# A roll along the columns: row pieces moved from two hardware DMA queues to the software ring

## The chip, the cores and the metric

The kernel runs on one core of one Trainium2 chip. The core has compute engines (TensorE, VectorE = DVE, ScalarE = ACT, GpSimd = POOL, and SyncE = SP, which only issues and waits) and 16 DMA engines that move data between the chip's main memory (HBM) and the core's working memory (SBUF), or from HBM to HBM. A DMA is issued by an instruction of SP, ACT or POOL, goes into that engine's queue, and is carried out by the DMA engines. The metric is the device time of one execution in microseconds. Before the change the median of three runs is 828.71 us (828.44 to 829.27).

## The reference

`x` is a float32 matrix of 8192 x 8192, `shift` is 100:

```python
def reference(x, shift):
    return np.roll(x, shift, axis=1)
```

So each output row is the input row turned by 100 places: `out[r, 100:] = x[r, :8092]` and `out[r, :100] = x[r, 8092:]`. There is no arithmetic; 268.44 MB are read and 268.44 MB are written.

## The kernel before

With `s = 100`, `a` is the next multiple of 128 above it, 128, and `g = a - s = 28`. Each output row is made of two parts.

*The long piece*: `out[r, 128:]` is `x[r, 28:8092]`, 8064 elements or 32,256 bytes. It goes from HBM to HBM directly (line L41). The rows are cut into 128 blocks `c` of 64 rows, and a block's row is named by `e` (0 to 15) and `j` (0 to 3): row `64c + 4e + j`. For each block there is one DMA for each `j`, over all 16 `e`, so that each of the 16 DMA engines gets one row of it. SP issues those with even `j`, ACT those with odd `j`. In the last four blocks each row is cut at column `mid = 4096`, and each half has a DMA of its own. SP and ACT issue 264 DMAs each: 248 of 504 KB, and 16 of 248 or 256 KB. On each of the two queues four DMAs are in flight: the next waits until the one four before it has landed.

*The head*: `out[r, :128]`, 512 bytes, is the end of row `r` (100 elements) followed by its beginning (28 elements). These go through SBUF, in 16 stages `k` of 512 rows, each partition `p` holding four successive rows `q`. Since the end of one row and the start of the next lie side by side in memory, one load (L70, tile `t`) reads 128 elements across each of the three row borders inside a partition's four rows. The end of the fourth row (L71) and the start of the first (L74) are loaded by themselves into the tile `h`. DVE copies the parts of `t` to their places in `h` (L72: ends, L75: starts). After all 16 stages of loads, 16 stores (L78) write the heads, `h` to `out[:, :128]`. All of these DMAs are issued by POOL, on the software ring, and are marked `single_packet=True`.

The order on POOL is the order of the program. Its ring has eight semaphores, taken in turn, so each POOL DMA waits until the one eight before it has landed; a store also waits for DVE's copies. Tiles have a buffer for each stage, so nothing waits for a buffer. SP's and ACT's queues and the POOL ring are independent of each other, since heads and long pieces write different bytes.

The queues have these names in the profile: q1 and q10 are the two hardware queues (SP's and ACT's; q10 is the one that began first, with ACT), q0 is the software ring of POOL, and q14 loads the program.

Of the kernel before, what the change touches and what calls it, by code (L numbers as in the profile page):

```python
# [1 line left out]

# [4 lines left out]


@with_exitstack
def kernel(  # L10
    ctx: ExitStack,
    tc: tile.TileContext,
    x: bass.AP,
    shift: int,
    out: bass.AP,
):
    nc = tc.nc
    n_rows, n_cols = x.shape
    s = shift % n_cols
    a = -(-s // 128) * 128  # L20
    g = a - s
    P = nc.NUM_PARTITIONS
    engines = [nc.sync, nc.scalar]
    n_chunks = 16
    rows = n_rows // n_chunks

    xm = x.rearrange("(c e j) w -> c j e w", e=16, j=4)
    om = out.rearrange("(c e j) w -> c j e w", e=16, j=4)
    if a < n_cols:
        blocks = n_rows // 64
        mid = (a + n_cols) // 256 * 128
        for c in range(blocks):
            parts = ((a, mid), (mid, n_cols)) if c >= blocks - 4 and a < mid else ((a, n_cols),)
            for j in range(4):
                for lo, hi in parts:  # L40
                    engines[j % 2].dma_start(out=om[c, j, :, lo:hi], in_=xm[c, j, :, lo - s:hi - s])  # L41
    if a == 0:
        return


    if a > 512:
        for i in range(n_chunks):
            r = slice(i * rows, (i + 1) * rows)
            nc.gpsimd.dma_start(out=out[r, :s], in_=x[r, n_cols - s:])
            if g > 0:  # L50
                nc.gpsimd.dma_start(out=out[r, s:a], in_=x[r, :g])
        return

    Q = 4
    n_st = n_rows // (P * Q)
    reads = ctx.enter_context(tc.tile_pool(name="reads", bufs=n_st))  # L60
    heads = ctx.enter_context(tc.tile_pool(name="heads", bufs=n_st))
    xt = x.rearrange("(k p q) c -> k p q c", q=Q, p=P)
    ot = out.rearrange("(k p q) c -> k p q c", q=Q, p=P)
    tiles = []
    for k in range(n_st):
        t = reads.tile([P, Q - 1, a], x.dtype)
        h = heads.tile([P, Q, a], x.dtype)
        lead = bass.AP(tensor=x.tensor, offset=(k * P * Q + 1) * n_cols - s,
                       ap=[[Q * n_cols, P], [n_cols, Q - 1], [1, a]])
        nc.gpsimd.dma_start(out=t[:], in_=lead, single_packet=True)  # L70
        nc.gpsimd.dma_start(out=h[:, Q - 1, :s], in_=xt[k, :, Q - 1, n_cols - s:], single_packet=True)  # L71
        nc.vector.tensor_copy(h[:, :Q - 1, :s], t[:, :, :s])  # L72
        if g > 0:
            nc.gpsimd.dma_start(out=h[:, 0, s:], in_=xt[k, :, 0, :g], single_packet=True)  # L74
            nc.vector.tensor_copy(h[:, 1:, s:], t[:, :, s:])  # L75
        tiles.append(h)
    for k, h in enumerate(tiles):
        nc.gpsimd.dma_start(out=ot[k, :, :, :a], in_=h[:], single_packet=True)  # L78


# [1 line left out]
_INS = ['x', 'shift']  # L82
_OUTS = [((8192, 8192), 'float32')]

_NUMBERS = {'shift': 100}


# [26 lines left out]
```

## Time and profile before

| | before |
|---|---|
| median of the runs | 828.71 us (828.44 to 829.27) |
| span of the profiled execution (first to last instruction) | 818.3 us |
| around the span, against the median | 10.4 us |
| POOL busy | 41.1 us |
| DVE busy | 7.8 us |
| data moved by the DMA engines | 272.71 MB, mean 333 GB/s |
| HBM traffic, read and written | 536.9 MB, 656 GB/s over the span |
| one POOL issue: L70, L71, L74, L78 | 759, 558, 538, 712 ns |
| issue to landing: rows of 504 KB, heads `t`, stores of `h` | 12.5, 32.6, 63.0 us (medians) |

The profiled execution's own device time is not listed beside the others; its span is 818.3 us, and it is compared with the median of the runs. In the list of the queues, the share is the time that a queue's packets took, as a part of 16 engines' time; a row of windows has the stretch and its length, the busy time of DVE and POOL with their instructions, the granted clock, the DMA engines' busy share and the rate in GB/s. A row that goes from HBM to HBM counts once in the DMA rate and twice in the HBM traffic (read and write). A row of waits has who waited for what, the total in us, how often, and the longest.

### The profile page before, as it was taken

Reading aid. Unit: us, or ns where it says so; the run is one execution under the profiler, and the core shown is the slowest. Engines: PE = TensorE matmul, PEld = TensorE weight load, DVE = VectorE, ACT = ScalarE, POOL = GpSimd, SP = SyncE. Lnnn points to the kernel's source line nnn. Section 1 sums busy time; section 2 is a strip of 40 time slices with the busy share of each in tenths; the row PEclk is TensorE's granted clock in tenths of the full one; section 3 lists DMA queues with packets and bytes.
Section 4 is the critical chain, followed back from the end, with each engine's and each line's share of the span. In section 5 each row is a group of like instructions: output and inputs, shape, how many; then the busy total and the mean of one; then the engine's idle time right before and its main releaser. Section 6 shows DMA issues by size and latency. Waiting matters only on the chain. (4 is left out here: it accounts for less than half of the span.)

```text
span 818.3 us, 689 instructions
## 1 busy us (share of the span) xinstructions
DVE 7.8 (1%) x32; POOL 41.1 (5%) x68
## 2 busy tenths in 40 slices
DVE  0000000000000000000000000000000000000000
POOL 3011111111010000000000000000000000000000
DMA  9999999999999999999999999999999999999998
GB/s 304 340 344 338 341 334 345 341 346 350 353 352 357 347 332 321 335 328 326 333 330 323 330 331 330 331 326 333 330 328 334 333 330 339 328 333 334 328 318 294
DMA packets 20229, 272.71 MB, mean 333 GB/s; under 512 B 9472, under 2 KB 9728, under 8 KB 11776
## 3 DMA queue, kind: packets, MB, share of 16 engines
q1 hardware_dynamic: 8448, 132.14, 48.2%
q10 hardware_dynamic: 8448, 132.14, 46.1%
q0 software_dynamic: 3328, 8.39, 4.7%
q14 instruction: 5, 0.04, 0.0%
HBM read 268.44 MB, written 268.44 MB: 656 GB/s over the span
## 5 line engine op out<-in xcount | busy, mean ns | idle before, releaser
L78 POOL DMA_DIRECT2D out_dram<-h x16 | 11.4, 712 | 87.2 <-DMA out_dram<-h 51.7
L70 POOL DMA_DIRECT2D t<-in_x_dram x16 | 12.1, 759 | 32.1 <-DMA h<-in_x_dram 31.3
L74 POOL DMA_DIRECT2D h<-in_x_dram x16 | 8.6, 538 | 85.7 <-DMA t<-in_x_dram 85.7
L71 POOL DMA_DIRECT2D h<-in_x_dram x16 | 8.9, 558 | 23.9 <-DMA h<-in_x_dram 23.9
L72 DVE COPY h<-t 128x300 f32<-128x300 f32 x16 | 5.9, 368 | 190.4 <-DMA t<-in_x_dram 190.4
L75 DVE COPY h<-t 128x84 f32<-128x84 f32 x16 | 3.2, 201 | 0.0
L95 POOL MEMSET const-float32-0.0<- 128x1 f32 x1 | 0.1, 99 | 0.2 <-issue 0.2
L95 POOL MEMSET const-bfloat16-1.0<- 128x1 bf16 x1 | 0.1, 101 | 0.0
L95 POOL MEMSET const-uint8-127<- 128x1 uint8 x1 | 0.1, 99 | 0.0
L95 POOL MEMSET const-float32-1.0<- 128x1 f32 x1 | 0.1, 98 | 0.0
## 6 DMA issues: line engine op xcount, KB each, us to landing
out_dram<-in_x_dram ACTq DMA_DIRECT2D x248, 504.0 KB, 12.5
out_dram<-in_x_dram SPq DMA_DIRECT2D x248, 504.0 KB, 12.5
out_dram<-h POOLq DMA_DIRECT2D x16, 256.0 KB, 63.0
t<-in_x_dram POOLq DMA_DIRECT2D x16, 192.0 KB, 32.6
out_dram<-in_x_dram SPq DMA_DIRECT2D x8, 256.0 KB, 5.9
out_dram<-in_x_dram ACTq DMA_DIRECT2D x8, 256.0 KB, 5.8
out_dram<-in_x_dram SPq DMA_DIRECT2D x8, 248.0 KB, 6.1
out_dram<-in_x_dram ACTq DMA_DIRECT2D x8, 248.0 KB, 6.1
```

The source lines that it names most:

```text
L70: nc.gpsimd.dma_start(out=t[:], in_=lead, single_packet=True)
L71: nc.gpsimd.dma_start(out=h[:, Q - 1, :s], in_=xt[k, :, Q - 1, n_cols - s:], single_packet=True)
L72: nc.vector.tensor_copy(h[:, :Q - 1, :s], t[:, :, :s])
L74: nc.gpsimd.dma_start(out=h[:, 0, s:], in_=xt[k, :, 0, :g], single_packet=True)
L75: nc.vector.tensor_copy(h[:, 1:, s:], t[:, :, s:])
L78: nc.gpsimd.dma_start(out=ot[k, :, :, :a], in_=h[:], single_packet=True)
L95: nc = _bacc.Bacc("TRN2", target_bir_lowering=False, num_devices=1)
```

## The change

All DMAs are now issued by POOL on the software ring; SP and ACT issue none. The long pieces of a block of 64 rows are one DMA, `[16, 4, 8064]`, marked as a single packet: each DMA engine gets four successive rows. There are 128 of these, of 2,016 KB each. The last blocks are no longer cut in halves. The heads keep their stages, loads, copies and stores, but they are woven between the long pieces: in each stage `k` of 512 rows come one long-piece DMA, the three loads of the heads, seven long-piece DMAs, and the store of the heads of stage `k - 2` (`lag = 2`). After the last stage the two stores that are left follow. POOL issues 192 DMAs in all, each of which waits for the one eight before it.

```diff
-    engines = [nc.sync, nc.scalar]
...
-    xm = x.rearrange("(c e j) w -> c j e w", e=16, j=4)
-    om = out.rearrange("(c e j) w -> c j e w", e=16, j=4)
-    if a < n_cols:
-        blocks = n_rows // 64
-        mid = (a + n_cols) // 256 * 128
-        for c in range(blocks):
-            parts = ((a, mid), (mid, n_cols)) if c >= blocks - 4 and a < mid else ((a, n_cols),)
-            for j in range(4):
-                for lo, hi in parts:
-                    engines[j % 2].dma_start(out=om[c, j, :, lo:hi], in_=xm[c, j, :, lo - s:hi - s])
+    J = 4
+    xm = x.rearrange("(c e j) w -> c e j w", e=16, j=J)
+    om = out.rearrange("(c e j) w -> c e j w", e=16, j=J)
+    blocks = n_rows // (16 * J)
+
+    def long_pieces(c):
+        if a < n_cols:
+            nc.gpsimd.dma_start(out=om[c, :, :, a:], in_=xm[c, :, :, a - s:n_cols - s], single_packet=True)
...
     Q = 4
     n_st = n_rows // (P * Q)
+    per = blocks // n_st
+    lag = 2
...
-    tiles = []
-    for k in range(n_st):
+    def read_heads(k):
         t = reads.tile([P, Q - 1, a], x.dtype)
         h = heads.tile([P, Q, a], x.dtype)
...
-        tiles.append(h)
-    for k, h in enumerate(tiles):
-        nc.gpsimd.dma_start(out=ot[k, :, :, :a], in_=h[:], single_packet=True)
+        return h
+
+    tiles = []
+    for k in range(n_st):
+        long_pieces(k * per)
+        tiles.append(read_heads(k))
+        for i in range(1, per):
+            long_pieces(k * per + i)
+        if k >= lag:
+            nc.gpsimd.dma_start(out=ot[k - lag, :, :, :a], in_=tiles[k - lag][:], single_packet=True)
+        if k == n_st - 1:
+            for m in range(n_st - lag, n_st):
+                nc.gpsimd.dma_start(out=ot[m, :, :, :a], in_=tiles[m][:], single_packet=True)
```

The loads and copies inside `read_heads` are those of before, unchanged.

More of the change, by code (lines that the diff above doesn't have):

```diff
@@ L22 @@
     P = nc.NUM_PARTITIONS
-    engines = [nc.sync, nc.scalar]
-    n_chunks = 16
-    rows = n_rows // n_chunks
-    xm = x.rearrange("(c e j) w -> c j e w", e=16, j=4)
-    om = out.rearrange("(c e j) w -> c j e w", e=16, j=4)
-    if a < n_cols:
-        blocks = n_rows // 64
-        mid = (a + n_cols) // 256 * 128
-        for c in range(blocks):
-            parts = ((a, mid), (mid, n_cols)) if c >= blocks - 4 and a < mid else ((a, n_cols),)
-            for j in range(4):
-                for lo, hi in parts:
[L41 to L49, printed above, removed]
+    J = 4
[5 more added lines that the diff above has]
+            nc.gpsimd.dma_start(out=om[c, :, :, a:], in_=xm[c, :, :, a - s:n_cols - s], single_packet=True)
+    if a == 0 or a > 512:
+        for c in range(blocks):
+            long_pieces(c)
+            r = slice(c * 16 * J, (c + 1) * 16 * J)
+            if s > 0:
+                nc.gpsimd.dma_start(out=out[r, :s], in_=x[r, n_cols - s:])
             if g > 0:
```

## The prediction

> **What bounds the kernel now.** I read the page first: the share of the engines and of the 16 DMA engines, then the queues.
>
> ```profile
> span 818.3 us, 689 instructions
> DVE 7.8 (1%) x32; POOL 41.1 (5%) x68
> DMA  9999999999999999999999999999999999999998
> q1 hardware_dynamic: 8448, 132.14, 48.2%
> q10 hardware_dynamic: 8448, 132.14, 46.1%
> q0 software_dynamic: 3328, 8.39, 4.7%
> HBM read 268.44 MB, written 268.44 MB: 656 GB/s over the span
> ```
>
> No compute engine matters; the DMA engines are busy from end to end (48.2 + 46.1 + 4.7 = 99%). That is not yet a bound: a packet's time contains what it waits for. So, second, the windows and the queues by window (columns of a queue: packets, MB, share of 16 engines).
>
> ```profile
> 2.00:20.00 18.00, 0.48 (x2) 6.06 (x11) 1.00 1.00 331
> 20.00:170.00 150.00, 5.83 (x24) 22.19 (x37) 1.00 0.99 340
> 200.00:265.00 65.00, 0.00 (x0) 6.39 (x9) 1.00 1.00 353
> 300.00:780.00 480.00, 0.00 (x0) 0.00 (x0) 1.00 1.00 330
> 780.00:800.00 20.00, 0.00 (x0) 0.00 (x0) 1.00 0.90 315
> 800.00:817.00 17.00, 0.00 (x0) 0.00 (x0) 1.00 0.94 314
> ```
>
> Of 20 to 170 us (heads are loaded beside the rows), then 200 to 265 (heads are stored), 300 to 780 (rows alone), 802 to 816 (half rows alone), and 2 to 4 (the first rows):
>
> ```profile
> q1 hardware_dynamic: 1476, 23.94, 44.0%
> q10 hardware_dynamic: 1456, 23.36, 39.9%
> q0 software_dynamic: 1804, 3.73, 15.4%
> ...
> q1 hardware_dynamic: 634, 10.19, 46.2%
> q10 hardware_dynamic: 638, 10.36, 43.5%
> q0 software_dynamic: 715, 2.34, 10.4%
> ...
> q1 hardware_dynamic: 4912, 79.23, 50.5%
> q10 hardware_dynamic: 4912, 79.23, 49.2%
> ...
> q1 hardware_dynamic: 282, 2.18, 49.5%
> q10 hardware_dynamic: 281, 2.31, 49.0%
> ...
> q10 hardware_dynamic: 20, 0.52, 83.1%
> ```
>
> A row piece is read from HBM and written to HBM, a head crosses HBM once in each of its two steps. So HBM moved 2 x 47.30 + 3.73 = 98.3 MB in 150 us, 656 GB/s; then 2 x 20.55 + 2.34 = 43.4 MB in 65 us, 668 GB/s; then 2 x 158.46 + 0.07 = 317 MB in 480 us, 660 GB/s. The DMA figure changes by stage (340, 353, 330), the HBM traffic does not. And an engine is not at its own limit: a row of the ACT queue (q10) took 39.9% x 16 x 150 us / 23.36 MB x 32,256 B = 1.32 us while heads were loaded, 49.2% x 16 x 480 / 79.23 x 32,256 B = 1.54 us without. So I take the bound to be the memory, at 656 to 668 GB/s, with some 12% of room on each engine (1.32 against the mean of 1.50).
>
> Third, who waits for whom.
>
> ```profile
> SPq L41 <- DMA out_dram<-in_x_dram: 671.1, 260, 4.8
> POOL out_dram L78 <- DMA out_dram<-h: 51.7, 7, 9.1
> ```
>
> SP waits for an earlier DMA of its own nearly all the time: the queues are full and issuing is free. Rows land 12.5 us after their issue (page, part 6), four DMAs deep on each queue, so no engine can be more than about 8 rows ahead of the slowest. POOL's ring is eight DMAs deep.
>
> **The change, part by part.** All sums start from the profiled execution's 818.3 us; the median of the runs is 828.71, so 10.4 us lie around the span (program load before the first instruction), and I leave that unchanged.
>
> 1. *Issue.* 512 row pieces leave as 128 DMAs of 64 rows instead of 528 on SP and ACT. SP's and ACT's issues cost nothing now (they wait 671 us), so taking them away gives 0. On POOL one such issue is bounded by its own rows: 0.54 us (L74) to 0.76 (L70); I take 0.6. 128 x 0.6 + 41 = 118 us in 818, while each 64-row DMA (2.06 MB) lasts 6.2 us at 330 GB/s. Hidden by the full ring: 0.
>
> 2. *Waits on POOL.* Each DMA now waits for the one eight before it, and everything queues behind that wait. In the new order any eight neighbours hold at least four row DMAs (store, three head loads, row DMAs for the rest), so at least 3 x 6.2 = 18 us of work is queued when a wait ends, against 0.6 us to issue. The store of head k-2 also waits for DVE (0.37 + 0.20 us of copies), whose loads were issued a stage of 8 x 6.2 = 50 us earlier. 0.
>
> 3. *Heads on the same ring, spread over the run.* The bytes are the same. At their own pace heads take 15.4% x 16 x 150 / 3.73 = 99 us of engine time per MB, 8.39 MB x 99 / 16 = 52 us an engine at most (the page's 4.7% gives 38), and rows at 1.32 us need 512 x 1.32 = 676; 728 together is under 818, so the engines still wait for memory. 0, as long as engines reach their heads at different times.
>
> 4. *Packets of four rows, a quarter of the completions.* Bounds from the half rows: there a row took 2 x 16,128 B at 2.18 MB / (49.5% x 16 x 14 us) = 19.7 and 2.31 / (49.0% x 224) = 21.0 GB/s, 1.59 us against 1.50 whole. If all of the 0.09 us is the price of one more packet and its completion, three of four saved give 512 x 3/4 x 0.09 = 35 us. At the other end it is nothing: that window is 14 us near the end, at 4.49 x 2 / 14 = 641 GB/s, and windows of that length swing as much (315 at 780 to 800, 331 at 2 to 20, where rows are whole). If the memory is the bound, saved engine time returns as waiting. I take 0 and keep 35.
>
> 5. *One ring instead of three.* No row in this trace follows another row of its own ring, so overlap within a ring is not shown. Below, a gain could only be the packet price of step 4, already kept there. Above, each row could cost what the first ones did, with nothing fetched ahead: 83.1% x 32 us = 26.6 us for 16 rows, 1.66 us. Then 512 x 1.66 + 38 + 6 = 894. I take 0, since the first rows also hold the cold start, and keep the end.
>
> 6. *Start.* The first row packet is at 2.14 us, 1.40 us after ACT's issue at 0.74. POOL's first issue is at 1.28 us and its first packet at 5.07, behind one row of each other queue. So the start moves by 1.28 + 1.40 - 2.14 = 0.5 to 5.07 - 2.14 = 2.9 us; I take 1.5. The Trainium skill (DMA: Bandwidth & Descriptors, Latency and other measured facts) puts the first byte at about 1 us on the software path and 0.6 on the hardware path; by it the start would move by 0.54 + 0.4 = 0.9 us and the sum would be 0.6 lower.
>
> 7. *End.* Now the last four blocks go in halves, which shrinks the window and draws the engines together: 315 instead of 330 GB/s for 20 us and 314 for 17 cost (15 x 20 + 16 x 17) / 330 = 1.7 us. Afterwards nothing does. The last instruction waits for the DMA eight before it, with five row DMAs (20 rows an engine) and three stores behind: an engine may finish as much as 20 x 1.32 + 3 x 0.76 = 28.7 us after the first (a store: 10.4% x 1040 us / 2.34 MB x 16 KB = 0.76). Bounds 0 and 28.7. The landings of one row DMA spread now over 6 to 8 us of the 12.5, half the window; half of 28.7 is 14 us of lag, evenly spread over the engines 7 us of work each. Together that is 7 x 16 x 24.4 GB/s / 330 = 8.3 us of memory time, but the last engine needs 14: a loss of 5.7. I take +5.7 - 1.7 = +4.0 (-1.7 to +27).
>
> Sum: 818.3 + 1.5 + 4.0 = 823.8 us of span, 834.2 of device time, +0.7%.
>
> **The rivals.** 0.2% (1.7 us) is about what can be told from no change.
>
> *Faster: the packet costs.* If a packet and its completion hold the engine for up to 0.09 us and the engine, not the memory, sets the pace, step 4 pays in full: 834.2 - 35 = 799. For it: 99% busy, half rows slower. Against it: 656 to 668 GB/s in every stage. It decides from 5.5 us on, that is 0.014 us a row.
>
> *Slower: engines drift to the edge of the window.* If one or two engines are steadily slower, the deep ring lets the others run off, and the end costs the full 27: 857. For it: POOL's eight-deep ring shows waits of 9.1 us between stores. Against it: the 12% of room that lets a late engine catch up. The Trainium skill has such a rule (same page and section): engines 7 and 15 are usually slower, its best guess being traffic to the software path's descriptor rings. No view here separates the engines.
>
> *Much slower: a ring does not overlap its rows.* Step 5: 894 of span, 904. Against it: the rate would have to fall below what the whole trace shows for queued rows.
>
> *No change.* If the engines stay within a few us, start and end cancel (+1.5 - 1.7): about 829. That the grouping does nothing is part of this and of the forecast: the packet records of q0, issued as single packets already, are of 4 KB, with rows of other queues between.
>
> **How the numbers follow.** Forecast 0.38, its own range 830.4 to 842; faster 0.27 (799 to 827); no change 0.10 (827 to 830.4); drift 0.12 (842 to 858); no overlap 0.13 (858 to 904). So faster 0.27, same 0.10, slower 0.38 + 0.12 + 0.13 = 0.63. The range leaves out no overlap (0.13) and the lower quarter of faster (0.07): 806 to 858.
>
> **What would show it.** Step 1: POOL about 118 us busy, its waits on earlier DMAs long. Steps 3 to 5: HBM 656 to 668 GB/s in the middle windows, and a row near 1.5 us on q0; under 1.45 speaks for packet costs, 1.6 or more for a ring that does not overlap. Step 6: the first window short by some 1.5 us of work. Step 7: the last 20 us fall off in steps of idle engines. The forecast is wrong if the middle rate moves by over 1%, which is 8 us.

## The result and the profile after

The change makes the kernel slower: 871.57 us median (852.17 to 879.3, four runs) against 828.66 us for the kernel before in runs beside it. The changed kernel's runs lie far apart, and the ratio is taken over those within 1.5% of the quickest, here two of the four: 1.035, with a 95% interval of 1.028 to 1.043, or some 29 us. By the medians it is 1.052.

One correction belongs ahead of the comparison. The profiled execution of the changed kernel took 864.1 us with a span of 862.3, so only 1.8 us lie around a span. The 10.4 us that the prediction set around the span of the kernel before were mostly another thing: with 1.8 us around its span of 818.3, its profile is from an execution of about 820 us. Beside the experiments the kernel before ran in 818.2 us on one chip and in 828.9 and 830.3 us on another, 1.3% apart. So the two profiles are compared by shares and shapes, and times on the chip of the changed kernel's runs: there a span of the kernel before is some 828.66 - 1.8 = 826.9 us, and the changed kernel's is 35.4 us longer.

The page of the changed kernel:

```profile
span 862.3 us, 285 instructions
DVE 7.8 (1%) x32; POOL 106.8 (12%) x196
DMA  9999999999999989999999999999989999899991
q0 software_dynamic: 13568, 272.64, 95.0%
HBM read 268.44 MB, written 268.44 MB: 623 GB/s over the span
```

POOL is still far from being the bound. But the DMA engines are no longer busy throughout: 95% instead of 99%, with two places where it is lost. The windows show both (length, busy time of DVE and POOL, clock, share of the DMA engines, GB/s):

```profile
2.00:20.00 18.00, 0.48 (x2) 6.26 (x12) 1.00 1.00 335
20.00:170.00 150.00, 0.97 (x4) 15.98 (x30) 1.00 1.00 329
170.00:300.00 130.00, 1.45 (x6) 16.86 (x30) 1.00 0.98 330
...
300.00:780.00 480.00, 4.37 (x18) 60.00 (x108) 1.00 0.96 320
780.00:836.00 56.00, 0.48 (x2) 6.82 (x12) 1.00 0.98 325
836.00:842.00 6.00, 0.00 (x0) 0.00 (x0) 1.00 0.87 318
842.00:858.00 16.00, 0.00 (x0) 0.00 (x0) 1.00 0.11 43
858.00:862.00 4.00, 0.00 (x0) 0.00 (x0) 1.00 0.00 0
```

Up to 170 us the engines are full. From then on 2 to 4% of their time is empty, although POOL waits most of the time (the two longest rows alone make 475 us) for an earlier DMA to land, that is, with its ring full:

```profile
POOL out_dram L31 <- DMA out_dram<-in_x_dram: 388.4, 76, 6.9
POOL t L57 <- DMA out_dram<-in_x_dram: 86.6, 15, 6.7
```

And from 842 to 858 us a rate of 43 GB/s at a share of 0.11 is one or two engines of sixteen at work. What happens is seen in the times at which the sixteen engines report one DMA done; the trace doesn't say which engine a report is from. These are the landings of single row DMAs, each in us after its first one, sorted:

```
kernel before, DMA of one row an engine, first landing at 592 us
  0.0 0.4 0.6 0.9 1.0 1.0 1.5 2.5 4.5 5.2 5.4 5.5 5.5 5.5 5.6  6.9
changed kernel, DMA of four rows an engine, first landing at 116 us
  0.0 0.5 0.6 0.7 1.3 1.5 1.7 1.8 1.9 3.4 3.5 3.7 4.6 4.8 9.5 12.6
at 209 us
  0.0 1.3 2.1 2.3 2.5 2.7 3.5 4.2 4.3 4.5 4.6 4.9 5.1 6.7 17.1 20.1
at 601 us
  0.0 0.0 0.1 0.3 0.4 0.4 0.6 0.7 1.1 1.1 1.5 1.6 1.7 2.3 5.8 22.0
at 815 us
  0.0 0.0 0.2 0.6 0.9 0.9 1.1 1.3 1.3 1.4 1.6 2.0 2.2 2.3 2.8 20.9
```

One engine, at first two, falls behind, within some 100 us, to about 20 us (16 to 25 over all DMAs from 170 us on), and stays there. I call it the straggler, and take the last landing of each DMA as its own: an engine 20 us behind can't make that up within a DMA of some 6 us, so it is the same engine from one DMA to the next. That distance is the depth of the ring: a DMA is issued only when the one eight before it has landed everywhere, and the prediction had counted at least 18 us of work in that window. So the other engines run into its edge, wait for the straggler, and at the end, from 842 us on, it has some 16 us of work left when the others have none. Its last rows, alone, take 1.194 us each.

The same trace shows what the straggler loses its time with. Steps between its landings, by kind of DMA, against those of the bunch (means over the 31st to the 185th DMA, when it is behind):

```
                       t load   100-element load   28-element load   head store   row DMA
straggler                2.93               1.61              0.20         1.48      5.89
median of the others     0.56               0.24              0.21         0.85      6.37
```

Heads cost it 6.2 us a stage, the others 1.9; at rows it is not slower, and the others' 6.37 us contain their waits for it. Eight row DMAs and the heads of a stage make 8 x 5.89 + 6.2 = 53.3 us for the straggler, and sixteen such stages 853 us: its own work fills the run.

The packet records say which short pieces are slow. I take those that start last before the straggler's landing as its own (means over twelve stages). In the `t` loads they are 4,096 bytes long and took 1.12 us, where the bunch's took 0.23; in the 100-element loads, 3,200 bytes, 1.58 us against 0.20. In the stores, again 4,096 bytes, they took 0.26 us against 0.18. So it is the two longer loads that are slow beside the other engines' rows: a packet with an eighth of a row's bytes takes three quarters of a row's time (1.53 us), or all of it.

What this costs is read from the HBM traffic, since an engine's idle time costs nothing while the others keep the memory busy. The DMA queue from 20 to 170 and from 300 to 780 us:

```profile
q0 software_dynamic: 2323, 49.28, 99.9%
...
q0 software_dynamic: 7645, 153.68, 96.1%
```

By the packets' lengths 48.25 and 148.96 MB of these are rows, which cross HBM twice, and the rest heads. That makes (2 x 48.25 + 1.03) / 150 = 650 GB/s and then (2 x 148.96 + 4.73) / 480 = 630. The kernel before on this chip has 536.9 MB in 826.9 us, 649 GB/s. So nothing is lost up to 170 us, nor up to 300 (651 GB/s). Against 650 GB/s the loss is 14.4 us from 300 to 780, 0.8 to 836, and 15.2 in the lonely end from 836 to 858. The last landing is at 857.9, and from there to the end of the span it is 4.4 us instead of 1.0, of which more below; the start costs 0.5. Together that is 34.3 of the 35.4 us.

### The profile page after: what moved, and what is told of

Its sections match the earlier page's. It is cut to its first block, busy times and chain, and to the rows that moved or that the text cites. A ratio compares the mean times of both kernels' runs of the same rounds, so it can differ in the third digit from the quotient of the medians.

```text
span 862.3 us, 285 instructions
## 1 busy us (share of the span) xinstructions
DVE 7.8 (1%) x32; POOL 106.8 (12%) x196
## 2 busy tenths in 40 slices
DMA packets 13570, 272.66 MB, mean 316 GB/s; under 512 B 3072, under 2 KB 3328, under 8 KB 5376
## 3 DMA queue, kind: packets, MB, share of 16 engines
q0 software_dynamic: 13568, 272.64, 95.0%
## 4 chain that ended last, share of the span: by engine, by line
DMA 95%; issue 1%; POOL 0%; POOLq 0%; PEldq 0%
DMA out_dram<-in_x_dram 63%; DMA t<-in_x_dram 32%; POOL out_dram L31 0%; POOL t L57 0%; POOLq L106 0%; POOL h L58 0%; POOL h L61 0%; PEldq L106 0%; POOLq L75 0%
## 5 line engine op out<-in xcount | busy, mean ns | idle before, releaser
L31 POOL DMA_DIRECT2D out_dram<-in_x_dram x128 | 64.5, 505 | 456.8 <-DMA out_dram<-in_x_dram 388.4
L72 POOL DMA_DIRECT2D out_dram<-h x14 | 10.4, 743 | 1.0 <-issue 0.4
## 6 DMA issues: line engine op xcount, KB each, us to landing
h<-in_x_dram POOLq DMA_DIRECT2D x16, 50.0 KB, 34.3
```

The lines of the kernel that those rows point to most:

```text
L31: nc.gpsimd.dma_start(out=om[c, :, :, a:], in_=xm[c, :, :, a - s:n_cols - s], single_packet=True)
L72: nc.gpsimd.dma_start(out=ot[k - lag, :, :, :a], in_=tiles[k - lag][:], single_packet=True)
```

## The experiments

All are edits of the changed kernel, and ratios are to the kernel before on the same chip.

**Everything on SP's hardware ring.** The edit, in all DMAs:

```diff
-nc.gpsimd.dma_start(...)
+nc.sync.dma_start(...)
```

> The changed kernel with every DMA issued by SP on its hardware ring: same order, same sizes, same eight-deep window, nothing on POOL. In the changed kernel's trace one engine lands each row DMA some 20 us after the other fourteen or fifteen, from 180 us on to the end, the others wait for it (DMA share 0.96) and it finishes 22 us alone. Theory A (the software ring slows one engine): no straggler here, HBM 655 to 665 GB/s in the middle, no lonely end, 826 to 838 us. Theory B (any single ring eight deep drifts like this): the straggler is there, 850 to 875 us. Theory C (long pieces of four rows are slow by themselves): also 850 or more, but with all engines alike.

Measured: 879.63 us against 818.19, ratio 1.067 (1.062 to 1.072). That is above what I had given for theory B, too. The straggler is there, in the rows from 150 us on 12 to 17 us behind. Of its page, and of its window from 300 us:

```profile
DMA packets 29698, 272.66 MB, mean 309 GB/s; under 512 B 7168, under 2 KB 21504, under 8 KB 21504
q1 hardware_dynamic: 29696, 272.64, 93.2%
```

```profile
300.00:780.00 480.00, 3.88 (x16) 0.00 (x0) 1.00 0.94 309
```

Theory A falls: the software ring is not the cause, and on the hardware ring the loss is not smaller. The packets say one thing more: the same transfers made 13,568 packets on the software ring and 29,696 here. The software ring groups the heads' short pieces into packets of up to 4,096 bytes, the hardware ring moves them in packets of 512, 400 and 112 bytes, though they are marked `single_packet` on both.

**The last blocks cut in halves**, as they were before the change:

```diff
-            nc.gpsimd.dma_start(out=om[c, :, :, a:], in_=xm[c, :, :, a - s:n_cols - s], single_packet=True)
+            if c < blocks - 4:
+                nc.gpsimd.dma_start(out=om[c, :, :, a:], in_=xm[c, :, :, a - s:n_cols - s], single_packet=True)
+            else:
+                for j in range(J):
+                    for lo, hi in ((a, 4096), (4096, n_cols)):
+                        nc.gpsimd.dma_start(out=om[c, :, j, lo:hi], in_=xm[c, :, j, lo - s:hi - s], single_packet=True)
```

> The changed kernel with the last four blocks cut into half rows, as before the change, all on the software ring, so that the window shrinks to eight half rows at the end. If the loss at the end is one of the wide window (step 7 of the prediction: engines apart when the work runs out), the last engine ends within 5 to 8 us of the others and the time falls by 13 to 17 us against the changed kernel, to 840 to 848 in its quick runs. If one slow engine sets the pace, it has the same rows to do, and the others only wait earlier: the lonely end goes, a slower stretch before it comes, and the time falls by 0 to 5 us.

Measured: 854.42 against 818.19, ratio 1.044 (1.042 to 1.046). This is the second of the two cases: the landings of the last DMA lie within 0.8 us, and yet there is no gain to be seen against the 1.035 and (below) 1.042 of the uncut kernel, which was not run on this chip and whose runs lie far apart. The windows show where the loss went:

```profile
300.00:780.00 480.00, 4.36 (x18) 60.06 (x108) 1.00 0.96 325
780.00:800.00 20.00, 0.00 (x0) 2.55 (x5) 1.00 0.94 321
800.00:820.00 20.00, 0.49 (x2) 2.91 (x6) 1.00 0.57 189
820.00:840.00 20.00, 0.00 (x0) 12.31 (x26) 1.00 0.84 285
```

From 800 to 820 us the engines are 0.57 busy: the others wait for the straggler there instead of after 840. A tighter end does not give back what an engine is behind; it has to do its rows either way.

**Rows alone.** Loads, copies and stores of the heads are left out, so the first 128 columns of the output are not written:

```diff
-        tiles.append(read_heads(k))
...
-        if k >= lag:
-            nc.gpsimd.dma_start(out=ot[k - lag, :, :, :a], in_=tiles[k - lag][:], single_packet=True)
...
```

> The changed kernel without the heads: their loads, DVE copies and stores are left out, so the first 128 columns of the output are not written. 528.5 MB of HBM traffic remain, 803 us at 658 GB/s, with start and end some 818 to 822 of device time. If the software ring itself makes an engine slow, the straggler is still there: 620 to 635 GB/s in the middle and a lonely end, 835 to 865 us. If the heads (short pieces, SBUF) in the same ring make it, it is gone: 815 to 824 us.

Measured: 821.37 against 818.19, ratio 1.004 (1.001 to 1.007). No straggler: the engines stay within 2 to 9 us of each other to the end.

```profile
300.00:780.00 480.00, 36.91 (x74) 1.00 1.00 330
812.00:817.00 5.00, 0.00 (x0) 1.00 0.00 0
```

330 GB/s is what the kernel before does with rows alone. So four rows of an engine in one DMA on one ring are neither better nor worse than single rows on two, and it is the heads in line with them that make the straggler. The second line is the end: the last landing is at 811.8 us, the span ends at 817.8.

**Row by row.** One DMA for each `j`, still on the software ring:

```diff
-            nc.gpsimd.dma_start(out=om[c, :, :, a:], in_=xm[c, :, :, a - s:n_cols - s], single_packet=True)
+            for j in range(J):
+                nc.gpsimd.dma_start(out=om[c, :, j, a:], in_=xm[c, :, j, a - s:n_cols - s], single_packet=True)
```

> The changed kernel with one DMA per row of an engine (16 rows each, 512 DMAs) on the software ring: the grouping of four rows is undone, the window shrinks to eight rows. If grouping or the wide window costs the time, this comes back to 826 to 836 us. If one engine is slow on the software ring whatever the grouping, the middle stays at 620 to 635 GB/s and only the lonely end shrinks, to some 6 to 8 us: 838 to 865 us. POOL issues 512 x 0.5 us more, 260 us in all, which is hidden either way.

Measured: 830.47 against 818.19, ratio 1.0145 (1.012 to 1.017).

```profile
300.00:780.00 480.00, 4.66 (x20) 172.59 (x340) 1.00 1.00 335
820.00:830.00 10.00, 0.00 (x0) 0.00 (x0) 1.00 0.10 38
```

The heads are in line as in the change, but the window is a quarter as deep, and no engine is more than 3 to 8 us behind. The engines are full (1.00, 335 GB/s against 325 for the cut end above, on the same chip with the same work). Most of the loss of the change is gone, then. This edit makes the DMAs smaller along with the window; since rows alone lose nothing by DMAs of four rows, I put it down to the window, but four-row DMAs with fewer in flight were not tried. Of the 12 us that remain, 3.5 are the end (last landing 825.3, end of the span 829.8, against 1.0 before).

**The change once more**, beside the kernels that follow:

> The changed kernel once more, beside the runs that it is compared with. The chip of the first experiments runs the kernel before in 818 us instead of 829. If the loss is a share of the time, 1.03 to 1.06 of the kernel before here too, with the same straggler some 20 us behind the others.

Measured: 877.89 us (864.01 to 886.4) against 828.92; 1.042 for the quickest run, 1.059 for the median. The straggler is 19 to 27 us behind, and the engines' share from 300 us on is a little lower still:

```profile
300.00:780.00 480.00, 3.88 (x16) 57.73 (x104) 1.00 0.95 312
```

**Heads on SP.** The edit, in `read_heads` and the stores alone:

```diff
-nc.gpsimd.dma_start(...)
+nc.sync.dma_start(...)
```

> The changed kernel with the heads' loads and stores issued by SP on its hardware ring; the row pieces stay on the software ring, four rows to an engine, eight DMAs deep. Rows alone on that ring had no straggler. If it is the heads standing in line with the rows that make one, it stays away here, HBM is at 655 to 665 GB/s in the middle and the time is 1.00 to 1.015 of the kernel before. If the heads make one engine slow wherever they stand, there is a straggler again and 1.03 or more.

Measured: 866.43 against 828.92, ratio 1.042 (1.036 to 1.048). This answered another question than the one asked. The page's queue and its issues, and the queue from 832 us to the end:

```profile
q1 hardware_dynamic: 19456, 8.39, 4.0%
...
t<-in_x_dram SPq DMA_DIRECT2D x16, 192.0 KB, 105.2
```

```profile
q1 hardware_dynamic: 7949, 3.53, 37.1%
```

The heads take 19,456 packets on this ring instead of 3,328, and a load needs 105 us to land, where it needed 33 before the change. (That each short packet waits its turn behind a row's packet would account for it, but the trace doesn't name the engines and so doesn't show it.) The heads fall behind the rows, and 3.53 of their 8.39 MB are moved after 832 us, when the rows are nearly done. Nor are the rows together: their landings spread over 20 us at 206 and 44 at 721 us, this time over all engines rather than with one straggler. That is more than rows show with no heads beside them (9 us above, 18 us in the next experiment). So a ring of its own does not keep the engines together when the rows' window is deep.

**Heads apart.** All loads after the first row DMA, all stores at the end, same ring:

```diff
+    long_pieces(0)
     for k in range(n_st):
-        long_pieces(k * per)
         tiles.append(read_heads(k))
-        for i in range(1, per):
-            long_pieces(k * per + i)
...
+    for c in range(1, blocks):
+        long_pieces(c)
+    for k in range(n_st):
+        nc.gpsimd.dma_start(out=ot[k, :, :, :a], in_=tiles[k][:], single_packet=True)
```

> The changed kernel with all head loads right after the first row DMA and all head stores at the very end, in the same software ring: the rows in between have no heads among them. In the changed kernel the straggler's heads of a stage take 2.93 + 1.61 + 0.20 us for the loads and 1.48 for the store, the others' 0.56 + 0.24 + 0.21 and 0.85. If its heads are slow because the others are busy with rows meanwhile, here all engines do heads together and quickly: 16 x 1.0 us of loads, 16 x 0.85 of stores, no straggler over 8 us in the rows, 1.03 to 1.04 of the kernel before, most of the loss now being memory that idles in the two blocks of heads. If one engine is slow at heads by itself, the loads alone take 16 x 4.7 = 75 us and the stores 24, 1.09 or more.

Measured: 865.28 against 828.92, ratio 1.045 (1.042 to 1.048), a little above the range.

```profile
10.00:42.00 32.00, 8.41 (x32) 28.60 (x49) 1.00 0.63 186
300.00:780.00 480.00, 0.00 (x0) 37.38 (x75) 1.00 1.00 325
846.00:862.00 16.00, 0.00 (x0) 7.31 (x10) 1.00 0.80 260
```

In the 48 loads, 10 to 37 us, no engine is more than 0.9 us behind the first: no engine is slow at heads when nobody does rows. The first stages, which were queued already, land 0.9 us apart, the later ones at POOL's pace of issue (28.6 us busy of 32), which I had not reckoned with. In the rows there is no straggler either, but four engines run ahead of twelve, by 12 us at 616 us, and from first to last it is 18 us in the end: rows drift apart by themselves too, at no loss here (share 1.00). The time is lost as expected, with the memory half idle in the heads: 186 GB/s for 32 us, and those are bytes that cross HBM once.

**Which engine?** The first of these kernels with everything on SP, and a small load more in eleven stages, which only `n` engines carry out:

```diff
+            if i == 4 and k in counts:
+                n = counts[k]
+                m = marks.tile([n, 1024], x.dtype)
+                nc.sync.dma_start(out=m[:], in_=x[k * 512:k * 512 + n, 0:1024])
```

> The changed kernel with everything on SP's hardware ring (the first experiment, which had the same straggler), and in eleven of the stages one small DMA more, a load of n rows of 4 KB into SBUF that only n of the 16 engines carry out (n = 8, 4, 12, 1, 2, 3, 5, 6, 7, 8, 9 in stages 4 to 14). A load whose n engines include the straggler has one landing some 12 to 20 us after the others; one that does not has none. If one certain engine is the slow one, the late landings appear from one n on and for all greater ones, the same in the first and in the later stages. If it is chance which engine falls behind, the pattern fits no single engine, or it changes between stages. 1.05 to 1.10 of the kernel before.

> As the marked kernel before (everything on SP's ring, a load by n engines in eleven stages), with n = 15, 14, 13, 12, 15, 14, 13, 12, 15, 14, 13 in stages 4 to 14. There the straggler was outside the n engines for every n up to 12. If it is one certain engine, each n here answers the same way in all its stages: late for 13 and above, 14 and above, 15 only, or never (then it is the one engine that only a DMA of all 16 uses). If it changes from program to program, n = 12 is late here, or the answers disagree.

Measured in the first, 893.33 us (one run): one straggler, 12 to 16 us behind in all eleven stages; the small loads never have a late landing, with any n up to 12. In the second, 881.87 us (one run): from stage 8 on two stragglers, some 11 to 14 and 13 to 17 us behind, and both are late in every small load, with n = 12 too. Three lines of each kind (us after the first landing of the row DMA ahead of it):

```
first, stage 6:    row DMA  ... 1.1  1.2  1.3  1.6 12.0     12 engines  0.3 0.3 ... 1.4 1.5 1.8
second, stage 11:  row DMA  ... 2.1  2.2  2.2  2.5 14.3 16.6     12 engines  0.2 0.3 ... 2.3 2.7 14.5 17.0
second, stage 4:   row DMA  ... 2.6  2.7  2.7 12.9 13.4 14.8     15 engines  0.2 1.7 ... 2.9 2.9 13.1 13.6 15.3
```

Both ran on one chip. If a DMA of twelve rows uses the same twelve engines in both, the straggler of the first is not one of the second's. The Trainium skill (DMA: Bandwidth & Descriptors, Why a DMA increments its semaphore by 16 and not by 1) says that on these rings it is the lowest-numbered ones, and that the sequencer makes up the rest of the count at once; the trace agrees with the latter, with one update 14 to 17 us ahead of the row DMA's first landing and then n others; which engines they are it doesn't show. Of the second program's three stragglers in stage 4 one had joined the bunch by stage 8. So, on that condition, which engine falls behind is not fixed, and one can catch up, but mostly it does not.

**Heads without SBUF**, copied from HBM to HBM:

```diff
-        tiles.append(read_heads(k))
+        r = slice(k * 512, (k + 1) * 512)
+        nc.gpsimd.dma_start(out=out[r, :s], in_=x[r, n_cols - s:], single_packet=True)
+        nc.gpsimd.dma_start(out=out[r, s:a], in_=x[r, :g], single_packet=True)
...
```

> The changed kernel with the heads copied from HBM to HBM, without SBUF and DVE: in each stage one DMA for the 100 elements and one for the 28 of 512 rows, in the place of the loads; same ring, same window, rows as in the change. If the straggler is an engine that is slow at short pieces to and from SBUF, it is gone: all engines within 10 us, 1.00 to 1.02 of the kernel before. If short pieces of any kind in line with the rows make it, it stays, with 15 to 25 us behind and 1.03 or more.

Measured: 870.47 against 830.34, ratio 1.047 (1.045 to 1.050).

```profile
300.00:780.00 480.00, 47.46 (x90) 1.00 1.00 313
```

No straggler, 12 us at most between the first and the last engine. The expected gain isn't there all the same: now all engines are busy and slower alike, a row 1.62 to 1.64 us, with 100 and 28 elements written to HBM in the place of full 512 bytes. Rows with the heads apart, on the same chip, took 1.58 us and ran at 325 GB/s.

**Loads without stores** (the first 128 columns are not written):

```diff
-        if k >= lag:
-            nc.gpsimd.dma_start(out=ot[k - lag, :, :, :a], in_=tiles[k - lag][:], single_packet=True)
...
```

> The changed kernel without the heads' stores: the loads and DVE's copies stay, the first 128 columns of the output are not written. In the changed kernel the straggler loses 2.4 + 1.4 us a stage on the loads and 0.6 on the store. If the loads make it, it is here as before, 15 to 25 us behind, and the time is that of the changed kernel less some 6 us of stores: 1.025 to 1.055 of the kernel before. If the stores make it, it is gone: 0.99 to 1.01.

Measured: 846.44 against 830.34, ratio 1.019 (1.017 to 1.021).

```profile
300.00:780.00 480.00, 4.39 (x18) 53.54 (x100) 1.00 0.98 323
820.00:841.00 21.00, 0.00 (x0) 0.00 (x0) 1.00 0.29 111
```

Some three stragglers, the last of them 17 to 30 us behind from 310 us on. The loads are enough to make them. The ratio lies under what I had expected, but the four runs reach from 845.53 to 870.18 us, too far apart to say what the stores add.

**Heads on 64 partitions** of eight rows:

```diff
-    P = nc.NUM_PARTITIONS
+    P = 64
...
-    Q = 4
+    Q = 8
```

> The changed kernel with the heads' tiles on 64 partitions of eight rows each, instead of 128 of four: the same 512 rows a stage, twelve pieces fewer to load separately for every sixteen, and each DMA engine serves other partitions. If the straggler's slowness belongs to the engine or to the short pieces, it stays 15 to 25 us behind, 1.03 to 1.06 of the kernel before. If it belongs to the SBUF partitions that this engine served (the upper 64), it is gone, 1.00 to 1.015.

Measured: 865.06 us (851.1 to 878.78) against 830.34, or 1.025 to 1.058 by run. Two to six engines are more than 8 us behind from 200 us on, the last of them 14 to 26 us. The straggler doesn't need the upper 64 SBUF partitions.

No kernel here beats the one before; of those that compute the whole output, row by row on the software ring comes nearest, at 1.0145.

## Why the prediction came out as it did

The sign was right, and 1.035 times the kernel before, 857.9 us, is at the very edge of the range; the median, 871.57 us, lies above it. The likeliest case, 834.2 us, was not what happened. It was another of the cases, engines that drift to the edge of the window, priced at 857 and given a chance of 0.12. The sign that the prediction had set for being wrong, a middle rate that moves by over 1%, came: 630 GB/s instead of 650.

- *The bound* (memory at 656 to 668 GB/s, room on each engine): borne out for the memory. Rows alone run at 330 GB/s whether grouped or not, one ring or two. The 12% of room was read from ACT's rows alone (1.32 us); SP's, by the row beside it, took 44.0% x 16 x 150 us / 23.94 MB x 32,256 B = 1.42, so over both queues it was some 9%. And the late engine didn't catch up with it.
- *Step 1, issue:* 106.8 us of POOL against 118 reckoned, a row DMA 505 ns against 600; hidden.
- *Step 2, waits on POOL:* taken as 0 because 18 us of work are queued when a wait ends. That held for the bunch as a whole, but an engine some 20 us ahead of the straggler has used these 18 us up. Measured: 2 to 4% of the engines' time from 170 us on, and by the HBM rate some 15 us. This is the term that I missed altogether.
- *Step 3, heads in the same ring:* 0 "as long as engines reach their heads at different times". This was the wrong way round. The bunch reaches its heads together and needs 1.9 us a stage; the engine that reaches them apart, while the others move rows, needs 6.2. I suppose that this feeds itself, since it then comes later still to the next heads; what first sets an engine back, in the first 100 us, no run here shows.
- *Step 4, packet costs:* 0 taken, 35 kept as the other end; it is 0 (rows alone at 330 GB/s).
- *Step 5, one ring:* 0 taken, and it is 0: the straggler's last rows follow each other in one ring at 1.194 us.
- *Step 6, start:* 1.5 us taken. The first row packet is at 2.63 instead of 2.14 us, the lower bound of 0.5.
- *Step 7, the end:* the step of the sum that failed most plainly. The bound of 28.7 us for one engine's lag was good, and 20.9 us were measured in it at 815 us. But I took half, evenly spread over the engines, from the landings of the kernel before, and it was one engine with nearly all: a loss of 15 us, against 5.7. The cause that the step gave was also too simple. Cutting the end in halves closed the gap, with no gain to be seen. And 3.4 us of the end I didn't see at all.

The drift case was right that engines drift to the edge of the window and that the last one works the end alone. That its 857 us came out is luck: it put 27 us at the end, where 15 were lost and 3.4 in what follows, and had nothing for the 15 us lost before, in the waits of step 2. Nor was it right about its condition: the straggler was not slow at rows (5.89 us against 6.37), and with rows alone there was none. The Trainium skill (DMA: Bandwidth & Descriptors, Latency and other measured facts), whose rule on engines 7 and 15 stood beside it, has traffic to the software path's descriptor rings as its best guess of the cause. Here a straggler appears on SP's ring as well, and, as far as the marked loads tell, it isn't always the same engine.

Shown by the runs: rows alone make no straggler; heads in line do, and their loads suffice; it appears on either kind of ring and with other SBUF partitions; with rows one by one, in a window a quarter as deep, most of its cost is gone. Shown by two programs, if a load of twelve rows uses the same engines in both: it is not one certain engine. Shown by the traces of the change, and by the heads apart from the rows: that the straggler's loads are slow only while the others do rows. What in the memory or in the engine makes a short load amid other engines' rows so slow was not tried, and stays open; so does why a deep window spreads the rows over all engines when the heads are on SP.

## What to carry to other kernels

Here the engines that share a DMA were held together by nothing but the waits of the queue: larger DMAs, with as many in flight and short loads among them, let them drift apart, and once they were apart by the whole window the slowest set the pace and worked the end alone. So before DMAs are made larger, look at the spread of the landings of one DMA, not only at the share of busy time. Where short loads stand among long rows, keep the window shallow: that was the only remedy here (1.0145), while a ring of their own for the heads (1.042), heads apart from the rows (1.045) and heads without SBUF (1.047) all lost as much as the change. A forecast for such a change has to ask what one late engine costs, not what the mean engine does.

## What the hardware showed that I had not expected

- When the software ring is used to the end, POOL's last drain ends some time after the last landing (in the change at 861.6 us, after 857.9): from the last landing to the end of the span it was 4.4 us in the change, 6.0 with rows alone, 4.5 row by row and 3.0 in the loads alone, against 1.0 in the kernel before (whose software ring had long been idle) and 0.8 with everything on SP.
- The same short transfers, marked as single packets, make 3,328 packets on the software ring and 19,456 on SP's, and beside long rows on another ring a load then takes 105 us to land, where it took 33 in the kernel before.
- A packet of 4,096 bytes from HBM into SBUF took 1.12 us for the engine that loaded heads while the others moved rows, and 0.23 for those that loaded together; one from SBUF to HBM took 0.26 and 0.18.
- Heads written to HBM in pieces of 400 and 112 bytes went with rows of 1.62 us and more on all engines, against 1.58 for rows without heads on the same chip, though they are 1.6% of the traffic.
- The kernel before takes 818.2 us on one chip and 828.9 to 830.3 on another.
